# A two-layer decoder step: sampled tokens' queries spread by repeated copies and full transposes, not through DRAM

## The chip, the cores and the metric

The kernel runs on one core of one Trainium2 chip. The metric is the device time of one execution in microseconds; the kernel before took 1097.1 us, the median of three runs from 1093.85 to 1100.27.

## What is computed

The reference is one inference step of two decoder layers over 256 prompt tokens and 32 sampled tokens (8 sequences of 4). Each layer has one input projection, dilated window attention in three groups of four heads beside a spatial gate, an output projection, cross-attention to 256 memory tokens, and an MLP. The sampled tokens attend to cached keys and values:

```python
def decoder_layer(x, pos, past_kv, mem_k, mem_v, p):
    proj = x @ p['w_in']
    q = rope_partial(proj[..., :a].reshape(B, T, N_ATT_HEADS, HEAD_DIM), pos)
    k = rope_partial(proj[..., a:2 * a].reshape(...), pos)
    ...
    for gi, (win, dil) in enumerate(DIL_PATTERNS):      # (128, 1), (512, 4), (2048, 16)
        past = past_kv[gi]
        kv_all = jnp.concatenate([past, new_kv], axis=1)
        o, lse = dilated_window_attention(q[:, :, hs], kv_all[:, :, 0], kv_all[:, :, 1], n_prefix, win, dil)
    ...
    mixed = jnp.concatenate([att, sgu], -1) @ p['w_mix_out']
    x = layer_norm(DEEPNORM_ALPHA * x + mixed, p['ln1_g'], p['ln1_b'])
```

## The kernel before

All activations are held transposed: features on partitions, 288 tokens (256 prompt, 32 sampled) along a row. TensorE multiplies each 128x128 block of a weight three times, since float32 is put together from high and low halves: `linear` issues L336, L337 and L338 for each of eight blocks, 24 matmuls for a part of 128 columns. The halves of the weights are made two parts ahead, `wh` on ScalarE (L318) and `wl` on VectorE (L319), from `wraw`, which SP's queue loads.

The first phase of a layer is the input projection: 22 parts, first the queries q0 to q5 and keys k0 to k5 (two parts to a group of four heads), then values and gate. The rotation of q and k goes over two engines: VectorE shuffles and multiplies (L671, L672), GpSimd multiplies and adds (L673, then L674, here its two halves). Beside `linear` run the attention's generators, which the class `Tasks` interleaves on TensorE by costs and latencies that each step yields. The program order so made, and the tile framework's own estimate of when operands are ready, set the order of each engine's queue; at run time every engine takes its queue strictly in order.

The change lies in `decode_scores`, the attention of sampled tokens to cached keys. For the dilated groups 1 and 2, `query(g)` lays the queries out so that partition (b, c) holds the four queries of sequence b: two narrow transposes (L989) into PSUM, a copy `qn` to SBUF (L991), a store to the DRAM tile `qd` from ScalarE's queue (L993), and a load from it into `qb` on SP's queue (L996), which repeats each sequence's 4 KB over 16 partitions. A cache tile `cu` is then multiplied by `qb`, on GpSimd (L1007) or VectorE (L1009), and VectorE sums over each head's 64 elements (L1010); `zs` (L1016) and 16 or 8 small matmuls (L1022) bring the scores into the softmax. `query(2)` is called after tile 4 of group 1. Cache tiles come through a stream of five buffers on SP's queue, keys first; a buffer is free when its sum is done. After the softmax, L1043 to L1051 transpose the probabilities and `decode_pv` multiplies them by the cached values (L1075), 13 of whose loads can only be issued as buffers come free there. The keys of a group are also transposed for the outputs (L752, L768) and used for prompt scores (L850, L854) and scores of new tokens (L949); these need the second half of the keys' rotation. The first input of the output projection that needs the decode attention is `attH` (L1111).

Of the kernel before, what the change touches and what calls it, by code (L numbers as in the profile page):

```python
# [9 lines left out]
F32 = mybir.dt.float32  # L10
# [60 lines left out]
def constants():  # L71
    """Tables that depend on the shapes alone."""
# [10 lines left out]
    n = np.arange(32)  # L83
# [22 lines left out]
class Null:  # L106
    """Stands in for the context while the order of the loads is recorded."""
# [17 lines left out]
class Stream:  # L125
    """Loads in the order in which they are asked for, issued ahead of their use."""
# [6 lines left out]
    def issue(self, n=1):  # L133
        """Up to n more loads, as far as there are free buffers."""
        if self.recording:
            return
        while n and self.issued < min(len(self.order), max(self.pos - 1, 0) + self.bufs):
            t = self.pool.tile(self.shape, F32, name=self.tag, tag=self.tag, bufs=self.bufs)
            for dst, src in self.source(t, self.order[self.issued]):
                self.nc.sync.dma_start(out=dst, in_=src)  # L140
            self.tiles[self.issued] = t
            self.issued += 1
            n -= 1
# [12 lines left out]
class Tasks:  # L156
    """Interleaves generators on the tensor engine's queue.

    A task yields (cost, latency): the tensor-engine time that it has just issued, and how long its next step
    has to wait for the results; or the name of a flag to wait for.  `now` is the time issued so far."""  # L160
# [54 lines left out]
def build(ctx, tc, I, O, worder, corder, recording):  # L215
# [4 lines left out]
    dp = ctx.enter_context(tc.tile_pool(name="dp", bufs=1, space=bass.MemoryType.DRAM))  # L220

    # ---- tiles
# [27 lines left out]
    # ---- loads  # L250
# [36 lines left out]
    def behind(ins, name):  # L287
        """Queues an instruction behind the latest urgent one of that engine."""
# [34 lines left out]
    def weights(key):  # L323
        """The next 128 columns, with the splits running two such parts ahead."""
# [16 lines left out]
    def linear(name, l, k0, tiles, H, L, N, evac, norm=None, folded=0, apply_at=1, ks=range(KT)):  # L341
        """tiles: column tiles of 256; evac(n, ps, bias) with n the index of the 128-column half.

        The first `folded` tiles run on the input that `norm` has not normalised yet."""
# [24 lines left out]
    # ---- constants  # L369
# [41 lines left out]
    def diag(z, base, outer, n_outer, inner, n_inner, last=1):  # L411
        """z flat: elements base + outer*i + inner*j + (0..last-1), as [p, i, j, last]."""
# [5 lines left out]
    if recording:  # L418
        diag = lambda *a: nc  # noqa: E731
# [3 lines left out]
    # ---- input  # L423
# [13 lines left out]
    # ---- layer norm parameters, one column per (norm, g or b, layer, tile)  # L437
# [30 lines left out]
    class LN:  # L468
        """z = xres + partial results, then the norm over all features of each token.

        The first two tiles give a first estimate c of the mean; sums run over z - c."""
# [9 lines left out]
        def fold_input(self, n):  # L481
            """(z - c) * g, and g and b as two more columns."""
# [14 lines left out]
        def fold(self, ps):  # L497
            """What the normalised input gives, without its constant, and the constant."""
# [73 lines left out]
        def apply(self, H, L=None):  # L572
            """x into xres and, if given, split into H and L."""
# [20 lines left out]
    class LastNorm:  # L594
        """z = xres + partial results, then the norm with tokens on partitions, into the outputs.

        The three token tiles start at 0, 128 and 160; of the last one only the sampled tokens count."""
# [58 lines left out]
    def gelu(dst, ps):  # L656
        """gelu(ps), tanh form: x * (1 + tanh u) / 2 = x / (1 + exp(-2 u))."""
# [21 lines left out]
    def layer(l, xH, xL, norm):  # L679
# [10 lines left out]
        # small per-layer parameters  # L690
# [55 lines left out]
        def natural(g, kv):  # L746
            """Keys or values of one head group, tokens on partitions, for the outputs (and P V)."""
# [33 lines left out]
        # ---- spatial gate  # L781
# [56 lines left out]
        # ---- prompt self-attention, two head slots at a time  # L838
# [70 lines left out]
        # ---- decode self-attention; score rows are 16 b + 4 t + h  # L909
# [14 lines left out]
        def decode_scores():  # L924
# [58 lines left out]
            def query(g):  # L983
                """The queries of one group on the partitions that hold keys of their sequence."""
                for pr in range(2):
                    yield f"q{2 * g + pr}"
                ps = tr()
                for pr in range(2):
                    T.transpose(ps[0:32, 128 * pr:128 * pr + 128], qT[:, 2 * g + pr, 256:288], ident)  # L989
                qn = sb.tile([32, 256], F32, name="qn", tag="qn", bufs=2)  # L990
                S.copy(qn, ps[0:32, 0:256])  # L991
                qd = dp.tile([32, 256], F32, name=f"qd{g}", tag=f"qd{g}", bufs=1)
                nc.scalar.dma_start(out=qd, in_=qn)  # L993
                qb[g] = sb.tile([128, 1024], F32, name="qb", tag="kt", bufs=2)
                src = qd.rearrange("(b t) c -> b (t c)", t=4)[:, None, :].to_broadcast([8, 16, 1024])
                nc.sync.dma_start(out=qb[g], in_=src)  # L996

            yield from query(1)
            yield 200, 4000
# [114 lines left out]
        # ---- phase 1: input projection  # L1114
# [25 lines left out]
        # ---- phase 2: output projection of the mixers  # L1140
# [21 lines left out]
        # ---- phase 3: keys and values of the memory, cross-attention  # L1162
# [46 lines left out]
        def values(h):  # L1209
            """Values of the memory for one head, memory tokens on partitions."""  # L1210
# [156 lines left out]
        # ---- phase 4: squared-ReLU MLP in four slices of the hidden width  # L1367
# [84 lines left out]
```

## Time and profile before

| | |
|---|---|
| median of three runs | 1097.1 us |
| runs | 1093.85 to 1100.27 us |
| span of the profiled execution | 1090.5 us (its own time is not given) |
| TensorE busy | 1045.1 us |
| VectorE, ScalarE, GpSimd busy | 767.2, 534.1, 191.2 us |

The span runs from the first to the last instruction that the profiler saw. An engine's row in a timeline gives the start, the duration, the operation with its tiles, and in brackets how long the engine had been idle before it and what ended that idle time. Matmuls overlap, so their starts, not their durations, tell their pace. Layer 0's input projection and decode attention lie at 20 to 145 us, layer 1's at 565 to 685 us.

### The profile page before, as it was taken

The page shows a single profiled execution, that of the slowest core. Times are in us where ns is not written, and L with a number is a line of the kernel's source. Part 1 is how long each engine was busy: PE and PEld are TensorE (multiplying, and loading weights), DVE is VectorE, ACT ScalarE, POOL GpSimd, SP SyncE. Part 2 cuts the span into 40 slices and gives each one's busy share as a digit, 9 for nine tenths or more (in the row PEclk, how much of TensorE's full clock was granted, in tenths as well). Part 3 has the DMA queues.
Part 4 walks back from the last instruction along what each step waited for, and adds up shares of the span by engine and source line. Part 5 has one row for each costly group of instructions (what it writes and reads, how often), then busy time and mean ns, then how long its engine had stood idle before and what let it go on. Part 6 is the DMA issues. An engine that isn't in the chain of part 4 may idle for free. (4 is left out here: it accounts for less than half of the span.)

```text
span 1090.5 us, 20141 instructions
## 1 busy us (share of the span) xinstructions
PE 1045.1 (96%) x8038; PEld 957.0 (88%) x8038; DVE 767.2 (70%) x1406; ACT 534.1 (49%) x1000; POOL 191.2 (18%) x151
## 2 busy tenths in 40 slices
PE   8989999999999999999978998999999999999995
PEld 7979599878898999999968885997788999999995
DVE  6688689755479756565998876895554997565656
ACT  4437456544457535353553373674343585354432
POOL 5592022000023000000469300220000320000000
PEclk9999999999999999999989999999999999999998
DMA  9988955687854655545446869456865555555531
GB/s 291 303 249 280 244 185 189 205 256 236 299 160 136 194 161 186 156 157 172 136 128 214 250 209 265 155 192 201 276 209 206 155 146 184 160 171 183 182 117 43
DMA packets 185533, 213.68 MB, mean 196 GB/s; under 512 B 5760, under 2 KB 175136, under 8 KB 185440
## 3 DMA queue, kind: packets, MB, share of 16 engines
q1 hardware_dynamic: 177216, 205.00, 59.9%
q10 hardware_dynamic: 8224, 7.41, 2.1%
q8 instruction: 63, 1.03, 0.4%
q14 instruction: 30, 0.25, 0.1%
HBM read 203.80 MB, written 8.59 MB: 195 GB/s over the span
## 5 line engine op out<-in xcount | busy, mean ns | idle before, releaser
L318 ACT ACTIVATE wh<-wraw 128x1024 fp32r<-128x1024 f32 (+1 forms) x237 | 249.4, 1054 | 294.9 <-PE acc L337 218.8
L319 DVE TENSOR_TENSOR wl<-wraw,wh 128x1024 fp32r<-128x1024 f32 (+1 forms) x237 | 309.1, 1306 | 113.2 <-ACT wh L318 112.1
L336 PE MATMUL acc<-xH,wh 128*128 128x288 f32 x728 | 218.5, 301 | 6.8 <-DVE fy L502 6.8
L338 PE MATMUL acc<-xH,wl 128*128 128x288 f32 x728 | 217.5, 299 | 3.3 <-DVE wl L319 3.3
L337 PE MATMUL acc<-xL,wh 128*128 128x288 f32 x728 | 217.5, 299 | 0.0
L336 PE MATMUL acc<-hH,wh 128*128 128x288 f32 x512 | 151.3, 296 | 0.0
L337 PE MATMUL acc<-hL,wh 128*128 128x288 f32 x512 | 151.2, 295 | 0.0
L338 PE MATMUL acc<-hH,wl 128*128 128x288 f32 x512 | 150.9, 295 | 0.0
L336 PEld LDWEIGHTS acc<-xH,wh 128*128 128x128 f32 x728 | 138.6, 191 | 8.2 <-issue 5.2
L338 PEld LDWEIGHTS acc<-xH,wl 128*128 128x128 f32 x728 | 138.5, 191 | 4.8 <-DVE wl L319 4.2
L337 PEld LDWEIGHTS acc<-xL,wh 128*128 128x128 f32 x728 | 138.6, 190 | 1.0 <-DVE fy L726 0.4
L520 POOL TENSOR_TENSOR s<-s,xres 128x288 f32<-128x288 f32 x15 | 20.3, 1353 | 464.4 <-DVE s L516 463.9
L336 PEld LDWEIGHTS acc<-hH,wh 128*128 128x128 f32 x512 | 96.3, 188 | 0.0
L337 PEld LDWEIGHTS acc<-hL,wh 128*128 128x128 f32 x512 | 96.3, 188 | 0.0
L338 PEld LDWEIGHTS acc<-hH,wl 128*128 128x128 f32 x512 | 96.2, 188 | 0.0
L336 PE MATMUL acc<-fH,wh 128*128 128x290 f32 x256 | 78.1, 305 | 1.8 <-DVE fy L502 1.8
L337 PE MATMUL acc<-fL,wh 128*128 128x290 f32 x256 | 77.0, 301 | 0.0
L338 PE MATMUL acc<-fH,wl 128*128 128x290 f32 x256 | 75.7, 299 | 0.5 <-DVE wl L319 0.5
L336 PEld LDWEIGHTS acc<-fH,wh 128*128 128x128 f32 x256 | 48.3, 189 | 2.6 <-PE acc L338 2.2
L337 PEld LDWEIGHTS acc<-fL,wh 128*128 128x128 f32 x256 | 48.5, 190 | 0.9 <-DVE fL L494 0.2
L338 PEld LDWEIGHTS acc<-fH,wl 128*128 128x128 f32 x256 | 48.1, 189 | 1.2 <-DVE wl L319 1.0
L1007 POOL TENSOR_TENSOR cu<-cu,qb 128x1024 f32<-128x1024 f32 x15 | 44.1, 2956 | 11.1 <-DMA qb<-qd 10.7
(318 smaller groups left out, 2199.4 us busy)
## 6 DMA issues: line engine op xcount, KB each, us to landing
cu<-cache_mem_kv SPq DMA_DIRECT2D x64, 512.0 KB, 6.2
wraw<-w_up SPq DMA_DIRECT2D x32, 1024.0 KB, 5.5
wraw<-w_down SPq DMA_DIRECT2D x32, 1024.0 KB, 4.9
cu<-cache_kv_w SPq DMA_DIRECT2D x48, 512.0 KB, 6.4
wraw<-w_in SPq DMA_DIRECT2D x21, 1024.0 KB, 6.7
wraw<-w_xkv SPq DMA_DIRECT2D x16, 1024.0 KB, 5.6
wraw<-w_mix_out SPq DMA_DIRECT2D x8, 1024.0 KB, 6.0
wraw<-w_xq SPq DMA_DIRECT2D x8, 1024.0 KB, 5.0
```

The costliest lines, as they stand in the source:

```text
L318: S.activation(h[:, r], raw[:, r], AF.Copy)
L319: gates[f"split{k}"] = behind(V.tensor_sub(lo[:, r], raw[:, r], h[:, r].bitcast(F32)), "dve")
L336: m = T.matmul(ps, wh[:, k], H[:, k], start=first, stop=False)
L337: T.matmul(ps, wh[:, k], L[:, k], start=False, stop=False)
L338: T.matmul(ps, wl[:, k], H[:, k], start=False, stop=last)
L520: eng.tensor_add(self.s, self.s, xres[:, n])
L1007: G.tensor_mul(cu, cu, qb[g])
```

## The change

`query(g)` no longer goes through DRAM. ScalarE writes each of the two query tiles of a group (128 features x 32 tokens) into a tile `qx` in which every column is repeated 16 times, ordered by token, sequence and copy (two copies of 128x512, in the shared staging buffers `stg`). Eight full 128x128 transposes of these into two PSUM tiles then give rows that are already repeated over the partitions, and two 128x512 copies on ScalarE put them into `qb`. The costs that are yielded to the interleaving change, and the DRAM pool `dp` is gone. Elsewhere in the file only comments and docstrings differ.

```diff
-    dp = ctx.enter_context(tc.tile_pool(name="dp", bufs=1, space=bass.MemoryType.DRAM))
...
             def query(g):
...
                 for pr in range(2):
                     yield f"q{2 * g + pr}"
-                ps = tr()
+                qb[g] = sb.tile([128, 1024], F32, name="qb", tag="kt", bufs=2)
+                qx = []
                 for pr in range(2):
-                    T.transpose(ps[0:32, 128 * pr:128 * pr + 128], qT[:, 2 * g + pr, 256:288], ident)
-                qn = sb.tile([32, 256], F32, name="qn", tag="qn", bufs=2)
-                S.copy(qn, ps[0:32, 0:256])
-                qd = dp.tile([32, 256], F32, name=f"qd{g}", tag=f"qd{g}", bufs=1)
-                nc.scalar.dma_start(out=qd, in_=qn)
-                qb[g] = sb.tile([128, 1024], F32, name="qb", tag="kt", bufs=2)
-                src = qd.rearrange("(b t) c -> b (t c)", t=4)[:, None, :].to_broadcast([8, 16, 1024])
-                nc.sync.dma_start(out=qb[g], in_=src)
+                    qx.append(stg("qx"))
+                    src = qT[:, 2 * g + pr, 256:288].rearrange("p (b t) -> p t b", t=4)
+                    S.copy(qx[pr].rearrange("p (t b c) -> p t b c", t=4, b=8),
+                           src[:, :, :, None].to_broadcast([128, 4, 8, 16]))
+                yield 0, 1200
+                for i in range(2):
+                    ps = tr()
+                    for j in range(4):
+                        t, pr = 2 * i + j // 2, j % 2
+                        T.transpose(ps[:, 128 * j:128 * j + 128], qx[pr][:, 128 * t:128 * t + 128], ident)
+                    S.copy(qb[g][:, 512 * i:512 * i + 512], ps)
+                yield 900, 0

             yield from query(1)
-            yield 200, 4000
+            yield 0, 1500
```

The engines' queues come out in another order at three places that matter below. In the changed file the lines up to the query stand one line higher (L672 and L673 are the two halves of the rotation on GpSimd there, L318 the split of weights on VectorE) and those after it four lower (L1011 and L1013 are the multiplications, L1014 the sum, L1020 `zs`).

On GpSimd in layer 0, around the first multiplications by the query tile. Before (qT from 509 and 510 is q4, from 571 and 572 q5; kT from 615 and 616 is k2, from 655 and 656 k3):

```order
L674 TENSOR_TENSOR qT_156<-ro_509,ro_510 128x288
L673 TENSOR_TENSOR ro_572<-ro_572,const_63 128x288
L674 TENSOR_TENSOR qT_156<-ro_571,ro_572 128x288
L673 TENSOR_TENSOR ro_616<-ro_616,const_63 128x288
L674 TENSOR_TENSOR kT_157<-ro_615,ro_616 128x288
L673 TENSOR_TENSOR ro_656<-ro_656,const_63 128x288
L674 TENSOR_TENSOR kT_157<-ro_655,ro_656 128x288
L1007 TENSOR_TENSOR cu_253<-cu_253,qb_432 128x1024
L1007 TENSOR_TENSOR cu_340<-cu_340,qb_432 128x1024
L1007 TENSOR_TENSOR cu_377<-cu_377,qb_432 128x1024
L1007 TENSOR_TENSOR cu_516<-cu_516,qb_432 128x1024
```

All rotations up to k3 stand ahead of the multiplications here. On GpSimd in layer 0, the same place now (q4 is 515 and 516, q5 577 and 578, k2 621 and 622, k3 661 and 662):

```order
L673 TENSOR_TENSOR qT_154<-ro_515,ro_516 128x288
L1011 TENSOR_TENSOR cu_251<-cu_251,qb_423 128x1024
L1011 TENSOR_TENSOR cu_338<-cu_338,qb_423 128x1024
L1011 TENSOR_TENSOR cu_375<-cu_375,qb_423 128x1024
L1011 TENSOR_TENSOR cu_522<-cu_522,qb_423 128x1024
L672 TENSOR_TENSOR ro_578<-ro_578,const_61 128x288
L672 TENSOR_TENSOR ro_622<-ro_622,const_61 128x288
L1011 TENSOR_TENSOR cu_583<-cu_583,qb_423 128x1024
L672 TENSOR_TENSOR ro_662<-ro_662,const_61 128x288
L673 TENSOR_TENSOR qT_154<-ro_577,ro_578 128x288
L673 TENSOR_TENSOR kT_155<-ro_621,ro_622 128x288
L1011 TENSOR_TENSOR cu_627<-cu_627,qb_423 128x1024
```

Four multiplications have moved ahead of the rotations of q5, k2 and k3, and a fifth ahead of the second halves of q5 and k2.

On VectorE in layer 1, around the first product and sums of group 2 (st_6909 before, st_6984 now). Before:

```order
L1009 TENSOR_TENSOR cu_6759<-cu_6759,qb_6757 128x1024
L1029 ISA dp_6437,dm_7108<-sc_6176,const_63 128x224
L1029 ISA dm_7108 128x1
L1010 TENSOR_REDUCE st_6909<-cu_6711 128x16
L319 TENSOR_TENSOR wl_6945<-wraw_6674,wh_6944 128x1024
L1016 TENSOR_TENSOR zs_6861<-st_6527,const_63 128x1024
```

The split `wl` stands behind group 2's product and its first sum. On VectorE in layer 1 now:

```order
L1014 TENSOR_REDUCE st_6549<-cu_6692 128x16
L1033 ISA dp_6451,dm_7195<-sc_6190,const_61 128x224
L1033 ISA dm_7195 128x1
L318 TENSOR_TENSOR wl_6945<-wraw_6696,wh_6944 128x1024
L1020 TENSOR_TENSOR zs_6928<-st_6549,const_61 128x1024
L318 TENSOR_TENSOR wl_7010<-wraw_6696,wh_7009 128x1024
```

Two splits and `zs` of group 1 have moved ahead of them.

On SP's queue in layer 1, around the last loads of cached values (w2048) and the memory's rows `mem_nat`. Before:

```order
L140 DMA cu_7512<-cache_kv_w2048 64x4x256 x2
L140 DMA cu_7554<-cache_kv_w2048 64x4x256 x2
L140 DMA cu_7575<-cache_kv_w2048 64x4x256 x2
L140 DMA cu_7582<-cache_kv_w2048 64x4x256 x2
L1142 DMA mem_nat_7643<-mem_prompt 128x2x1024
```

The memory's rows come last. On SP's queue in layer 1 now:

```order
L140 DMA cu_7591<-cache_kv_w2048 64x4x256 x2
L140 DMA cu_7598<-cache_kv_w2048 64x4x256 x2
L140 DMA cu_7605<-cache_kv_w2048 64x4x256 x2
L1146 DMA mem_nat_7673<-mem_prompt 128x2x1024
L140 DMA cu_7612<-cache_kv_w2048 64x4x256 x2
```

The load of the memory's rows has moved ahead of the last tile's two halves.

## Rows read from the trace of the kernel before

**Rows 1.** Page: span, then busy time, share and instructions of TensorE

```profile
span 1090.5 us, 20141 instructions
...
PE 1045.1 (96%) x8038; PEld 957.0 (88%) x8038; DVE 767.2 (70%) x1406; ACT 534.1 (49%) x1000; POOL 191.2 (18%) x151
```

**Rows 2.** Timeline of ScalarE, layer 0: start, us, engine, line, operation, out<-in [idle before]

```profile
34.53 0.36 ACT L991 COPY qn<-tr 32x256 f32<-32x256 f32 x1 [0.28 <-PE tr L989]
...
38.23 0.35 ACTq L993 DMA_DIRECT2D qd<-qn  x1
...
38.62 0.59 ACT L712 COPY wst<-tr 128x512 f32<-128x512 f32 x1 [3.73 <-PE sc L932]
```

**Rows 3.** Timeline of the SP queue, layer 0

```profile
44.30 0.71 SPq L996 DMA_DIRECT2D qb<-qd  x1
```

**Rows 4.** Timeline of GpSimd (POOL), layer 0

```profile
42.79 1.67 POOL L674 TENSOR_TENSOR qT<-ro 128x288 f32<-128x288 f32 x1
...
49.13 1.66 POOL L674 TENSOR_TENSOR kT<-ro 128x288 f32<-128x288 f32 x1
...
55.93 12.38 POOL L1007 TENSOR_TENSOR cu<-cu,qb 128x1024 f32<-128x1024 f32 x4 [1.93 <-DMA qb<-qd]
```

**Rows 5.** View of the tile qb: duration ns min/median/max; idle us before it, times

```profile
L1007 POOL TENSOR_TENSOR cu<-cu,qb x15: 2347/3362/3457, 55.9 to 615.6; 128x1024 f32<-128x1024 f32 x15
...
  DMA qb<-qd: 13.9, 5
```

**Rows 6.** Waits of TensorE, 20 to 145 us: us in total, times, longest

```profile
PE tr L752 <- POOL kT L674: 2.9, 2, 1.8
...
PE tr L850 <- DVE m L858: 0.7, 1, 0.7
```

**Rows 7.** Timeline of TensorE, layer 1

```profile
595.72 0.40 PE L989 MATMUL tr<-const,qT 128*32 128x128 f32 x1 [3.06 <-POOL qT L674]
...
596.15 0.44 PE L338 MATMUL acc<-xH,wl 128*128 128x288 f32 x1
...
596.39 0.44 PE L336 MATMUL acc<-xH,wh 128*128 128x288 f32 x1
...
619.12 0.61 PE L338 MATMUL acc<-xH,wl 128*128 128x288 f32 x1 [2.64 <-DVE wl L319]
...
676.38 0.64 PE L1075 MATMUL o<-cu,z 128*32 128x256 f32 x8 [1.64 <-DMA cu<-cache_kv_w]
```

**Rows 8.** Timeline of GpSimd, layer 1

```profile
575.67 1.67 POOL L674 TENSOR_TENSOR qT<-ro 128x288 f32<-128x288 f32 x1
...
578.93 9.17 POOL L1007 TENSOR_TENSOR cu<-cu,qb 128x1024 f32<-128x1024 f32 x3 [1.60 <-DMA qb<-qd]
...
595.63 0.80 POOL L674 TENSOR_TENSOR kT<-ro 128x288 f32<-128x288 f32 x1
```

**Rows 9.** Timeline of VectorE, layer 1

```profile
615.70 1.22 DVE L1010 TENSOR_REDUCE st<-cu 128x16 f32<-128x1024 f32 x1 [1.97 <-POOL cu L1007]
```

**Rows 10.** Timeline of TensorE, layer 0

```profile
44.18 0.38 PE L336 MATMUL acc<-xH,wh 128*128 128x288 f32 x1
...
57.07 0.38 PE L989 MATMUL tr<-const,qT 128*32 128x128 f32 x2
...
57.29 0.60 PE L752 MATMUL tr<-const,kT 128*128 128x128 f32 x4
...
57.72 0.38 PE L768 MATMUL tr<-const,kT 128*32 128x128 f32 x2
```

**Rows 11.** Busy times of a stretch, granted clock (PEclk), DMA share, GB/s

```profile
595.80:597.80 2.00, 2.00 (x10) 1.92 (x11) 2.00 (x5) 0.36 (x1) 1.92 (x3) 0.50 0.21 35
```

**Rows 12.** Timeline of the SP queue, layer 1

```profile
652.01 14.69 SPq L140 DMA_DIRECT2D cu<-cache_kv_w  x13
...
667.19 0.37 SPq L1142 DMA_DIRECT2D mem_nat<-mem_prompt  x1
```

**Rows 13.** Busy times in layer 1, DMA share and GB/s last

```profile
664.00:668.00 4.00, 4.00 (x26) 2.07 (x26) 3.04 (x13) 2.08 (x9) 0.00 (x0) 1.00 1.14 200
```

## The prediction

> **What bounds the kernel now.** I read the page first: TensorE is busy for 1045.1 of 1090.5 us [rows 1], so its queue is the length of the kernel, and only what lengthens that queue or leaves it idle counts. The profiled span lies 6.6 us under the median of 1097.1 us; the time of that execution itself is not given, so I add my sum, made against the span, to the median. Then I read TensorE's timeline over the two stretches in which the queries are spread (20 to 145 us in layer 0, 565 to 685 us in layer 1), for every idle time above 0.2 us and its releaser, then each releaser's own engine. The reader is to see three things.
>
> First, the removed chain is long. In layer 0 the copy of the queries stands at 34.53, its store is issued at 38.23 [rows 2], the load at 44.30 [rows 3], and GpSimd's first multiplication with it begins at 55.93 [rows 4]. Engines wait 13.9 us for these loads, in 5 places [rows 5].
>
> Second, hardly any of that is TensorE's. Its waits in layer 0 are 2.9 us for rotated keys and 0.7 us for VectorE [rows 6]. The rotated keys come from GpSimd, whose queue also holds the multiplications.
>
> Third, in layer 1 two waits do hang on the chain. TensorE waits 3.06 us for q5's rotation [rows 7], which stands on GpSimd behind multiplications that waited for the load until 578.93 [rows 8]. It waits 2.64 us for a weight split [rows 7], which stands on VectorE behind a sum that waited for GpSimd's product, 1.97 us, that had waited for group 2's load [rows 9]. Behind either wait the matmuls start 0.24 us apart [rows 7]; before, 96 of them took 44.18 to 57.07, 0.134 us each [rows 10]. The granted clock of that slow stretch is 0.50 [rows 11], so it is the lower of the two levels (1.2 for 2.4 GHz). By the spacing it lasts 10 to 12 matmuls, which at 0.106 us more each is 1.1 us behind the first wait and 1.25 behind the second.
>
> **The work added to TensorE.** Per layer 16 full transposes come and 4 narrow ones go. Four full ones start at 57.29 and the next instruction at 57.72 [rows 10], 0.11 each, so 16 cost 1.75. Two narrow ones take 0.22 (57.07 to 57.29 [rows 10]), so 4 give back 0.44. Three more breaks in the rows of matmuls at about 0.09 each add 0.27. Sum +1.6 us per layer, 3.2 in all, all on the path. A transpose here is dearer by the Trainium skill, TensorE: Matmul & The Clock Gate, Part 4: PE-mode transpose, which gives about 275 ns for one in a kernel (for bf16). By that figure 32 of them would cost 8.8 us and the forecast below would be 5.3 us longer; the rows above, at 0.11 in a row, speak against it, and I use them.
>
> The ScalarE copies (4 per group, 0.59 us for 128x512 [rows 2]) cost TensorE nothing: ScalarE is a part ahead with its splits. If that cover were gone, 16 copies would be 9.4 us. The copy of q5's queries waits on ScalarE for GpSimd's q5, with a split queued behind it; that split is wanted two parts, 6.4 us, later, so I take nothing. The stores and loads themselves (2 each per layer, 512 KB for each load) free SP's and ScalarE's queues; TensorE waited for neither, so nothing.
>
> **Layer 0: the order on GpSimd.** The scheduler, which now thinks that the query tile is ready early, moves four multiplications ahead of the rotations of q5, k2 and k3. Before, k2 is done at 50.8 [rows 4], long before TensorE wants it. Now it comes behind this row:
> - TensorE reaches the six transposes of group 1 at about 44.4 [rows 10] and needs 0.7; two copies follow on ScalarE between its other work: the query tile is ready at 46.2 (45.4 to 47.5), after q4's rotation has ended at 44.46 [rows 4].
> - Four multiplications: 12.4 us as before [rows 4], so to 58.6. Bounds: 4 x 2.35 = 9.4 and 4 x 3.46 = 13.8 [rows 5].
> - The first halves of q5 and k2, a fifth multiplication (2.35 to 3.46), k3's first half, then the second halves of q5 and k2. A half takes 0.81 to 1.67 us (1.66 and 1.67 in [rows 4], 0.80 in [rows 8]). Middle 8.4, ends 6.4 and 10.5. So k2 is there at 67.0 (61 to 71).
>
> TensorE gets to the group that needs k2 one part after 57.07 [rows 10]: 57.07 + 3.2 + 1.0 for eight transposes and two breaks = 61.3. It waits 5.7 us, and 1.2 for the clock behind it. k3 follows on GpSimd a sixth multiplication and two halves later, 4.9 us, while TensorE has 3.7 us of work: another 1.2. Sum 8.1, in place of the 3.6 of [rows 6] (k4 and k5, which now come before they are wanted): +4.5.
>
> Behind this, VectorE's sums wait for GpSimd's products with splits queued behind them. I walked that queue: the split that is wanted first comes 0.4 to 2 us before TensorE needs it, so +0.4, ends 0 and +2. With 1.6 of work layer 0 is at **+6.5** (-1.5 to +10) when the values of the caches begin; two pairs of prompt scores that move ahead of that point (0.42 each) leave the stretch behind it, so they cancel.
>
> The spread of 2.35 to 3.46 us for one multiplication [rows 5] has a rule beside it: the Trainium skill, SBUF — State Buffer, Who interferes with whom, says that GpSimd and a VectorE instruction with two SBUF inputs exclude each other for a whole instruction. By it the four would take 9.4 us if VectorE did only sums and waits in that time, and 13.8 if it split weights all along. The trace agrees with both ends, and VectorE has three splits in those 12 us as before, so the middle stays.
>
> **Layer 1.** GpSimd's order does not change, and q4's second half runs from 575.67 to 577.34 whatever the query does [rows 8]; the tile, ready at about 574, lets the multiplications start at 577.4 instead of 578.93. So all behind moves up 1.5 us, and no more: k2 (which ends at 596.43 [rows 8]) is there at 594.9, and TensorE, 0.8 later by added transposes, comes at about 593.4. It waits 1.5 instead of 3.06 and stays under the length at which the clock fell: -2.7. The second wait (2.64 and 1.25 for the clock behind it) goes, since VectorE now has the split ahead of group 2's products: -3.9. Work +1.6. Sum -5.0.
>
> What is late next: the values of the caches. TensorE ends that stretch with a wait of 1.64 us for the last of them [rows 7]. Thirteen loads are issued from 652.01 on, the memory's rows (1 MB) behind them at 667.19 [rows 12]. Now the memory's rows are issued ahead of the last tile. 1 MB at the 200 GB/s of that time [rows 13] would be 5.2 us; if the two share the engines, little. I take 2.5 (0 to 5). And three pairs of prompt scores (0.42 each) move ahead of the stretch, which loads bound, so 1.3 is not given back. Layer 1: -5.0 + 1.3 + 2.5 = **-1.2** (-5 to +2).
>
> **Sum.** +6.5 - 1.2 = +5.3; I take 5 us, so 1102 us.
>
> **Rivals.**
> - *Rotations not late, faster.* If the four multiplications take 9.4 and each half 0.8, k2 comes at 46.2 + 9.4 + 6.4 = 62.0: a wait of 0.7, none for k3. Layer 0 is then 0.7 + 1.6 - 3.6 = -1.3, layer 1, with the memory's rows hidden and the moved scores given back, -5.0: 1097.1 - 6.3 = 1091. For it: 2.35 us is on record [rows 5]. Against: three splits of VectorE fall in that time.
> - *Slower.* VectorE becomes the bound in layer 0: its sum of the first product waits for GpSimd, and k2's rotation on VectorE, two splits and the second sum stand behind it. It decides once the query tile comes later than about 48, when the split for the part at 58 is late: then 2 us more on TensorE, k2 later by the same 2, and with the memory's rows fully ahead (5 instead of 2.5) the sum is 5.3 + 2 + 2 + 2.5 = 11.8, so 1109; with one of these 1105 to 1107. For it: margins of 0.4 us in my walk. Against: the copies on ScalarE are short.
> - *It does not do what it says.* The products start no earlier, because the fifth cache tile or q4 holds GpSimd in both layers (as q4 does in layer 1). Then the order on GpSimd gives back about what layer 1 wins, and 3.2 us of work less 3 to 4 of the two old waits is left: 1096 to 1098.
>
> **How the numbers follow.** The forecast, 1102, has 0.43 with a range of its own of 1098 to 1106; the limit of +0.5% (about what a measurement here can tell from no change, 5.5 us) is 1102.6, so I put 0.30 of it within and 0.13 above. Faster rival 0.17. Slower rival 0.26, the dearer transposes 0.02. No effect 0.12. So faster 0.17, same 0.30 + 0.12 = 0.42, slower 0.13 + 0.26 + 0.02 = 0.41. For 8 in 10 the range leaves out the outer half of the faster rival and the outer third of the slower: 1090.5 to 1108.5.
>
> **What would show it.** In the changed kernel's timeline: GpSimd's four multiplications from about 46 to 59; k2's second half at 65 to 69; TensorE idle 4 to 7 us for GpSimd's keys near 61 to 67, with 0.24 us between the matmuls behind it; in layer 1 one wait of 1 to 2 us for k2 near 594, no wait for a split near 619, and a wait of 2 to 6 us for the last cache values near 674. A query tile later than 50, no wait near 61, or a wait for the split in layer 1 would make me wrong.

## The result, and the profile after

The changed kernel took 1116.51 us (median; 1114.37 to 1118.29), the kernel before beside it 1098.68 us (1093.85 to 1100.67): a ratio of 1.0158, 95% interval 1.0123 to 1.0193. It is slower by 1.6%, where 1102 us and at most 1108.5 were forecast. The profiled execution took 1115.4 us. Its page, against [rows 1]:

```profile
span 1113.7 us, 20180 instructions
...
PE 1063.1 (95%) x8062; PEld 972.0 (87%) x8062; DVE 770.3 (69%) x1406; ACT 541.2 (49%) x1012; POOL 187.5 (17%) x151
```

The span grew by 23.2 us, TensorE's busy time by 18.0: most of the loss is not idle time. Four stretches hold nearly all of it. They are cut at the same places of TensorE's queue in every kernel: in layer 0 from the 51st group of three matmuls of `linear` to the first multiplication with cached values, and from there to the 201st group; in layer 1 from the 977th group, and to the 1153rd. The view gives the busy time of each engine by stretch; the columns are the stretch, its length, the busy times, the granted clock (PEclk), DMA share and GB/s. The kernel before:

```profile
41.00:111.75 70.75, 67.08 (x497) 63.38 (x496) 60.13 (x114) 36.64 (x79) 41.62 (x21) 1.00 0.89 272
111.75:153.68 41.93, 39.35 (x331) 27.40 (x330) 26.80 (x93) 17.14 (x43) 0.00 (x0) 0.96 0.83 239
564.87:651.31 86.44, 80.12 (x595) 74.65 (x593) 72.50 (x132) 40.35 (x82) 41.30 (x26) 0.96 0.69 213
651.31:696.48 45.17, 42.33 (x351) 30.47 (x350) 30.10 (x97) 21.13 (x51) 1.86 (x2) 1.00 0.82 234
```

The changed kernel:

```profile
41.83:122.61 80.78, 76.38 (x521) 70.89 (x520) 61.91 (x120) 39.75 (x83) 38.21 (x21) 0.92 0.69 223
122.61:172.45 49.84, 42.57 (x322) 28.29 (x322) 25.74 (x85) 17.54 (x46) 0.00 (x0) 0.83 0.75 202
584.16:671.68 87.52, 85.22 (x618) 79.64 (x616) 75.59 (x140) 44.45 (x89) 40.92 (x26) 0.94 0.61 198
671.68:719.85 48.17, 41.34 (x338) 30.84 (x338) 27.99 (x88) 20.39 (x50) 1.87 (x2) 0.93 0.78 219
```

The length less TensorE's busy time is its idle time. The four stretches grew by 10.0, 7.9, 1.1 and 3.0 us, 22.0 in all; idle time accounts for +0.7, +4.7, -4.0 and +4.0, together 5.4, and busy time for the other 16.6. The added work was put at 3.2 us. The third column from the end tells where most of the rest is: the granted clock fell from 1.00, 0.96, 0.96 and 1.00 to 0.92, 0.83, 0.94 and 0.93. The levels are 1.00 and 0.50 (2.4 and 1.2 GHz), so twice what is missing from 1.00 is the share of a stretch at the lower one: by that 47 us of the four stretches, against 10 before.

TensorE's timeline in layer 0, where it waits for k2 (columns as in [rows 7]):

```profile
62.81 0.29 PE L336 MATMUL acc<-xL,wh 128*128 128x288 f32 x1
67.51 0.48 PE L751 MATMUL tr<-const,kT 128*128 128x128 f32 x1 [4.41 <-POOL kT L673]
...
70.54 0.44 PE L335 MATMUL acc<-xH,wh 128*128 128x288 f32 x1
70.78 0.44 PE L336 MATMUL acc<-xL,wh 128*128 128x288 f32 x1
...
76.05 0.38 PE L335 MATMUL acc<-xH,wh 128*128 128x288 f32 x1
```

and GpSimd's timeline ahead of it, which answers to [rows 4]:

```profile
46.92 11.46 POOL L1011 TENSOR_TENSOR cu<-cu,qb 128x1024 f32<-128x1024 f32 x4 [2.20 <-ACT qb L999]
58.33 2.55 POOL L672 TENSOR_TENSOR ro<-ro,const 128x288 f32<-128x288 f32 x2
60.84 2.40 POOL L1011 TENSOR_TENSOR cu<-cu,qb 128x1024 f32<-128x1024 f32 x1
...
65.69 1.77 POOL L673 TENSOR_TENSOR kT<-ro 128x288 f32<-128x288 f32 x1
```

So the mechanism stands as it was drawn: four multiplications from 46.92 to 58.38, k2's second half ending at 67.46, one wait of 4.41 us. Behind it the matmuls start 0.24 us apart (70.54, 70.78), not for ten of them but up to 75.3. The clock of that stretch and of one in the next, in the same columns as above:

```profile
65.10:75.30 10.20, 7.79 (x29) 6.97 (x30) 10.20 (x13) 1.11 (x3) 10.12 (x8) 0.50 0.74 240
133.40:147.00 13.60, 12.02 (x56) 5.11 (x55) 2.65 (x11) 4.08 (x12) 0.00 (x0) 0.50 1.13 203
```

The second of these follows three waits for cached values in a row, and one for `od`, the output of the decode attention on its way to `attH`, comes after it:

```profile
129.79 0.64 PE L1079 MATMUL o<-cu,zp 128*32 128x256 f32 x8 [0.89 <-DMA cu<-cache_kv_w]
132.42 0.64 PE L1079 MATMUL o<-cu,zp 128*32 128x256 f32 x8 [1.99 <-DMA cu<-cache_kv_w]
...
135.07 1.08 PE L1079 MATMUL o<-cu,zp 128*32 128x256 f32 x8 [1.47 <-DMA cu<-cache_kv_w]
...
156.05 0.41 PE L1100 MATMUL tr<-const,od 128*128 128x128 f32 x2 [2.12 <-DVE od L1093]
```

In layer 1 there is one wait for k2, none for a split, and a late last tile of cached values, with a wait for `attH` behind it; at 0.50 lie 614.62 to 621.45 and 699.96 to 706.78:

```profile
613.75 0.33 PE L751 MATMUL tr<-const,kT 128*128 128x128 f32 x1 [2.30 <-POOL kT L673]
...
698.60 0.64 PE L1079 MATMUL o<-cu,z 128*32 128x256 f32 x8 [2.69 <-DMA cu<-cache_kv_w]
...
703.18 1.09 PE L335 MATMUL acc<-attH,wh 128*128 128x288 f32 x3 [1.28 <-ACT attH L1115]
```

### The profile page after: what moved, and what is told of

It reads as the page before. It is cut to its first block, busy times and chain, and to the rows that moved or that the text cites. A ratio compares the mean times of both kernels' runs of the same rounds, so it can differ in the third digit from the quotient of the medians.

```text
span 1113.7 us, 20180 instructions
## 1 busy us (share of the span) xinstructions
PE 1063.1 (95%) x8062; PEld 972.0 (87%) x8062; DVE 770.3 (69%) x1406; ACT 541.2 (49%) x1012; POOL 187.5 (17%) x151
## 5 line engine op out<-in xcount | busy, mean ns | idle before, releaser
L318 DVE TENSOR_TENSOR wl<-wraw,wh 128x1024 fp32r<-128x1024 f32 (+1 forms) x237 | 307.4, 1300 | 121.7 <-ACT wh L317 121.1
L1011 POOL TENSOR_TENSOR cu<-cu,qb 128x1024 f32<-128x1024 f32 x15 | 40.5, 2723 | 24.2 <-ACT qb L999 24.2
```

What stands on the lines that cost most here:

```text
L318: gates[f"split{k}"] = behind(V.tensor_sub(lo[:, r], raw[:, r], h[:, r].bitcast(F32)), "dve")
L1011: G.tensor_mul(cu, cu, qb[g])
```

## The experiments

Two questions lead through them: what the waits and the clock behind them cost, and which of the change's two parts, the new way of the data or the new yields, brings them.

**GpSimd's rotations first.** The multiplications are held behind the rotations that the program asks for before them:

```diff
-        (G if ROPE[1] else V).tensor_add(dst, e, f)
+        gates["rope"] = (G if ROPE[1] else V).tensor_add(dst, e, f)
...
-                        G.tensor_mul(cu, cu, qb[g])
+                        behind(G.tensor_mul(cu, cu, qb[g]), "rope")
```

> The changed kernel, with one thing put back: a multiplication by the query tile on GpSimd is queued behind the rotations issued so far, so q5, k2, k3 and k4 stand between the first four multiplications. Theory (the late rotation of k2 is what costs layer 0): no wait of TensorE near 61 to 67, no slow clock there, layer 0's projection 7 to 9 us shorter than in the changed kernel, which took 1116.5; time 1106 to 1110. Rival (the transposes and copies themselves cost it, whatever GpSimd's order): the stretch stays within 2 us and the time at 1114 to 1118.

Measured: 1108.49 us, 1.0107 times before (1.0042 to 1.0172). The time lies where the theory had it, but the stretch does not. The wait of 4.41 us is gone, and others have come. The waits of TensorE in layer 0 (line, releaser: us in all, times, longest):

```profile
PE s L1026 <- DVE zs L1020: 2.9, 1, 2.9
PE tr L767 <- DVE m L857: 2.4, 1, 2.4
PE sc L948 <- POOL kT L673: 1.7, 1, 1.7
```

The stretch up to the cached values took 83.47 us, more than the 80.78 of the changed kernel. What this kernel gains lies behind it: 44.92 and 45.24 us in the second and fourth stretches, against 49.84 and 48.17. The edit moved more than GpSimd's queue there: the four prompt scores that the changed kernel leaves for layer 0's second stretch now stand ahead of it, and in layer 1 the memory's rows are loaded behind all loads of cached values again. So without the late rotation of k2 the first stretch is as long as with it; that GpSimd's order by itself is not the loss is shown further down, with the old yields.

**TensorE kept busy in the wait.** 46 matmuls whose result is overwritten stand ahead of k2's transposes in layer 0:

```diff
-            ps = tr()
+            ps = tr(); [T.matmul(ps[:, 0:288], xH[:, 0, 0:128], xH[:, 0], start=True, stop=True) for _ in range(46 if (g, kv, l) == (1, 0, 0) else 0)]
```

> The changed kernel with 46 useless matmuls of 128x288 (6.1 us at full clock) put on TensorE in layer 0 ahead of the transposes that need k2, to fill the wait of 4.4 us. Theory (most of that wait's price is the lower clock behind it, 10.2 us at half pace): the clock stays at its upper level from 61 to 75, and the projection of layer 0 gets 1 to 3 us shorter although 6.1 us of work are added. Rival (the clock would have fallen anyway, because of the row of short matmuls): the added work costs 1.7 us or more and a stretch at the lower level stays near 65 to 75.

Measured: 1113.43 us, 1.015 times before (1.0066 to 1.0234). TensorE's timeline at the wait, and the clock of the whole stretch:

```profile
57.81 6.23 PE L748 MATMUL tr<-xH 128*128 128x288 f32 x46
...
66.12 0.33 PE L751 MATMUL tr<-const,kT 128*128 128x128 f32 x1 [1.43 <-POOL kT L673]
...
67.80 0.29 PE L335 MATMUL acc<-xH,wh 128*128 128x288 f32 x1
67.93 0.29 PE L336 MATMUL acc<-xL,wh 128*128 128x288 f32 x1
...
71.59 0.38 PE L335 MATMUL acc<-xH,wh 128*128 128x288 f32 x1
```

```profile
42.00:119.60 77.60, 75.97 (x563) 71.11 (x563) 61.75 (x118) 39.88 (x83) 37.07 (x20) 1.00 0.70 223
```

The same instructions, from k2's first transpose to the part behind k3's, take 71.59 - 66.12 = 5.5 us at the full clock (0.2 of it a wait for k3) and 76.05 - 67.51 = 8.5 us in the changed kernel: the clock behind that wait cost 3.1 us, not 1.2. The stretch up to the cached values fell from 80.78 to 78.84 us although 6.1 us of work (57.81 to 63.87) was put in and its idle time shrank by no more than 2.8 (4.4 to 1.6). So the clock, at 1.00 in all of it and without the 13.6 us at 0.50 of the changed kernel, gave back some 5 us: 0.3 to 0.4 us for each us at the lower level. The Trainium skill, TensorE: Matmul & The Clock Gate, HAM oscillation — how this bites in real kernels, counts half of the time at the lower clock as lost. Behind this wait it was 3.1 of 10.2 us, so the measurement decides for less: 2.4 us of these had passed in the wait itself (65.1 to 67.5).

**The memory's rows last.** In layer 1 `mem_nat` had been issued between the loads of cached values:

```profile
672.38 9.83 SPq L140 DMA_DIRECT2D cu<-cache_kv_w  x11
682.27 0.60 SPq L1146 DMA_DIRECT2D mem_nat<-mem_prompt  x1
684.76 1.68 SPq L140 DMA_DIRECT2D cu<-cache_kv_w  x2
```

The load is put behind the last of them (the lines that keep hold of that load are left out):

```diff
...
-        nc.sync.dma_start(out=mem_nat, in_=I["mem_prompt"][0].rearrange("(a p) d -> p a d", p=128))
+        behind(nc.sync.dma_start(out=mem_nat, in_=I["mem_prompt"][0].rearrange("(a p) d -> p a d", p=128)), "g2.1")
```

> The changed kernel with the load of the memory's rows held behind the last load of cached values, as it stood before. Theory (the 1 MB ahead of the last tile costs layer 1's end): the wait of 2.69 us for the last values falls to about 1, the lower clock behind it goes, layer 1's end is 3 to 5 us shorter, time 1112 to 1114. Rival (those loads share the engines, so the order does not matter): layer 1's end stays within 1 us and the time at 1116.

Measured: 1106.58 us, 1.0092 times before (1.0057 to 1.0126). The SP queue:

```profile
668.49 14.09 SPq L140 DMA_DIRECT2D cu<-cache_kv_w  x13
683.13 0.37 SPq L1146 DMA_DIRECT2D mem_nat<-mem_prompt  x1
```

The fourth stretch fell from 48.17 to 44.92 us, below the 45.17 of before; the last wait for cached values is 1.73 instead of 2.69 us, and the one for `attH` is gone. So of the loss some 3 us by the trace hang on this one load. The median moved by 10 us, below what either theory had said; the traced execution took 1109.98, 3.4 more than the median, and its stretches of layer 0 are unchanged (80.36 and 49.60), so I don't put the rest of that down to the load.

**The yields of before.** The data path is the new one, the three yields are the old:

```diff
-                yield 0, 1200
...
-                yield 900, 0
...
             yield from query(1)
-            yield 0, 1500
+            yield 200, 4000
```

> The changed kernel with the costs and latencies that the query steps yielded before (one latency of 4000 behind the first query, none between copies and transposes). Theory (the order on GpSimd comes from the estimate of when the query tile is ready, not from these costs): the four multiplications still stand ahead of q5, k2 and k3, the wait near 61 to 67 stays 4 to 6 us, time 1112 to 1120. Rival (the smaller latency made the order): the wait goes and the time falls to 1106 to 1110.

Measured: 1091.95 us, 0.9952 times before (0.9922 to 0.9983): faster than the kernel before, by half a per cent. I had expected 1112 to 1120. The four stretches, from the fastest of its ten executions:

```profile
40.62:114.67 74.05, 69.28 (x514) 65.59 (x512) 63.47 (x112) 39.10 (x83) 39.21 (x21) 0.98 0.77 245
114.67:155.68 41.01, 38.92 (x331) 27.59 (x330) 27.15 (x93) 17.50 (x45) 0.00 (x0) 1.00 0.83 245
566.42:647.70 81.28, 78.58 (x598) 74.35 (x596) 72.97 (x130) 43.62 (x88) 41.71 (x26) 0.98 0.68 213
647.70:691.94 44.24, 41.38 (x359) 30.62 (x358) 30.55 (x100) 20.62 (x51) 1.86 (x2) 1.00 0.79 239
```

GpSimd still has the four multiplications ahead of k2's rotation, and nearly at the same times:

```profile
45.71 10.46 POOL L1009 TENSOR_TENSOR cu<-cu,qb 128x1024 f32<-128x1024 f32 x4 [2.20 <-ACT qb L998]
...
63.47 0.80 POOL L673 TENSOR_TENSOR kT<-ro 128x288 f32<-128x288 f32 x1
```

The first stretch has as much idle time as in the changed kernel (4.8 against 4.4 us), but in pieces of 2.35 us and less, and its clock is 0.98 against 0.92. On SP's queue the memory's rows come behind the cached values again, so that move came from the yields and not from the query's way. On TensorE 36 prompt-score matmuls stand ahead of the cached values in either layer, as before the change; the changed kernel has 44 in layer 0 and 48 in layer 1, and its transposes for group 2 in layer 0 stand 9 to 41 groups of three matmuls later.

**The old way of the data with the new yields.** The other corner of the square: the kernel before, with the three new yields at the same places.

```diff
+                yield 0, 1200
                 ps = tr()
...
                 nc.sync.dma_start(out=qb[g], in_=src)
+                yield 900, 0
...
             yield from query(1)
-            yield 200, 4000
+            yield 0, 1500
```

> The kernel before, store and load through DRAM kept, with the three yields of the change put at the same places of its generator (0, 1200 ahead of the transposes of the queries, 900, 0 behind the load, 0, 1500 in place of 200, 4000 after group 1). Theory (the yields, not the data path, make the time: they move pairs of prompt scores and the group's transposes to other places of TensorE's queue, which leaves less work between the cached values and more and longer stretches at the lower clock): slower than before by 0.8 to 2%, 1106 to 1120 us, with waits of over 4 us in all for the cached values and lower-clock stretches of over 25 us in the four stretches that the queries touch. Rival (the transposes and GpSimd's early multiplications make the time): within 0.5% of before, 1091 to 1103 us.

Measured: 1114.77 us, 1.0156 times before (1.0109 to 1.0204), just what the whole change costs, and within the theory's range. Its four stretches:

```profile
42.89:113.42 70.53, 69.27 (x518) 64.67 (x516) 62.61 (x121) 36.91 (x79) 40.84 (x21) 1.00 0.83 259
113.42:162.82 49.40, 39.23 (x312) 27.01 (x310) 24.63 (x82) 16.85 (x42) 0.00 (x0) 0.86 0.82 202
574.31:670.74 96.43, 84.04 (x611) 77.73 (x609) 74.96 (x142) 41.58 (x85) 39.95 (x26) 0.93 0.66 191
670.74:719.74 49.00, 40.81 (x336) 29.07 (x334) 27.90 (x87) 19.90 (x48) 1.86 (x2) 0.93 0.78 216
```

The loss looks different here: idle time is 1.3, 10.2, 12.4 and 8.2 us, 32.0 in all against 15.4 before, with the longest wait 5.22 us for cached values in layer 0, and the first stretch loses nothing. What the two kernels share are the second and fourth stretches (49.4 and 49.0 here, 49.8 and 48.2 in the changed kernel) and their lower clock.

**Each inner yield alone.** The changed kernel without the `yield 900, 0`, and without the `yield 0, 1200`. The third yield decides nothing: with 200, 4000 in its place beside the two inner ones, the queues of all engines are built the same.

> The changed kernel without its second yield (900, 0, behind the eight transposes of a group); 0, 1200 stays. The order on TensorE in layer 0 keeps the late place of group 2's transposes and the four more prompt-score matmuls ahead of the cached values; layer 1 has two of six back. Theory (the latency of 0, 1200 does most of it): 1108 to 1116 us. Rival (the cost of 900, which the planner takes for work that is not there, does it): 1090 to 1100 us.

> The changed kernel without its first yield (0, 1200, between the copies and the transposes of a group); 900, 0 stays. Group 2's transposes move forward and prompt scores stand as before the change. Theory (the latency does most of it): 1090 to 1100 us. Rival (the cost of 900 does it): 1108 to 1117 us.

Measured: 1104.95 us without the cost (ratio 1.0084, 1.0054 to 1.0115), 1110.08 without the latency (1.0134, 1.0086 to 1.0181). The first lies between the two theories' times, the second in the rival's: neither yield does it alone, and each of them alone leaves the kernel slower than before. Without the latency the prompt scores stand as before the change, and still the first stretch takes 81.2 us, with waits of 3.31 us for k2 and 2.85 for `zs`. So the moved scores are not the one cause either. The four stretches took 80.36, 50.38, 84.00 and 43.62 us without the cost, and 81.22, 44.92, 81.52 and 49.05 without the latency: in these traces taking the cost away shortens layer 1 alone, and taking the latency away the second and third stretches. Only with both do the memory's rows stand among the loads of cached values; without either one of them they come last.

**Both good edits together.** The yields of before and the memory's rows last.

> The changed kernel with the yields of before (none within the query, 200, 4000 after group 1) and with the memory's rows loaded behind the last tile of cached values. With the order by the old yields the kernel took 1091.95 us; the late load took 3 us off the wait at the end of layer 1 where the yields were the new ones. Theory (the two add): 1087 to 1091 us. Rival (with the old yields the memory's rows stand behind the last tile anyway or hide): 1090.5 to 1093.5 us, no difference.

Measured: 1089.64 us, 0.9957 times before (0.9932 to 0.9981). The median lies in the theory's range, but the ratio is that of the old yields alone, so nothing was added. With the old yields the memory's rows already stand behind the thirteen loads: there was nothing left to gain.

**The new yields in one layer.** `if l == 1:` (or `l == 0`) ahead of the new yields, the old ones in the other layer.

> The changed kernel with the yields of before in layer 0 and the new ones in layer 1 alone. With the old yields in both layers it took 1091.95 us, with the new in both 1116.51. Theory (each layer pays for its own order; by the two traces 15.5 us of the difference lie in layer 0 and 10.1 in layer 1): 1100 to 1104 us, with layer 0 as with the old yields (cached values from about 115 us on, first parts of the next stretch at 156) and layer 1 as in the changed kernel. Rival (the loss is one thing that starts in layer 0 and drags on): 1090 to 1094 us.

> The changed kernel with the new yields in layer 0 alone, those of before in layer 1. Theory (each layer pays for its own order): 1105 to 1109 us, the sum of its gain and that of the kernel with new yields in layer 1 alone is the whole difference of 24.6 us. Rival (loss starts in layer 0 and drags on): 1113 to 1118 us.

Measured: 1099.81 us with the new yields in layer 1 (ratio 1.0042, 1.0009 to 1.0074), just under the theory's range, and 1106.88 in layer 0 (1.0111, 1.0078 to 1.0145). Above the 1091.95 with none that is 7.9 and 14.9 us, 22.8 together, of the 24.6 with both (by the ratios 0.9 and 1.6%, 2.5 together, of 2.1). Each layer pays for its own order. The traces say it by stretch: with the new yields layer 0 took 80.38 and 48.64 us (80.78 and 49.84 in the changed kernel), with the old ones 74.05 and 42.48; layer 1 took 85.97 and 49.68 with the new (87.52 and 48.17), 82.53 and 47.68 with the old.

**Rotations first, with the old yields.** The edit of the first experiment on the kernel with the old yields.

> The changed kernel with the yields of before, and GpSimd's multiplications put behind the rotations of q and k that stand before them in the program, as in the kernel before. Theory (with the yields of before, GpSimd's order is not what costs; the wait that it takes away, 2.4 to 4.8 us in layer 0, is replaced by one for products or splits): 1089 to 1096 us. Rival (the multiplications ahead of the rotations still cost the waits and the clock behind them): 1083 to 1088 us.

Measured: 1091.81 us, 0.9967 times before (0.9945 to 0.999), against 1091.95 without the edit. So with the old yields GpSimd's order costs nothing. Once more one wait took the place of another: the longest of layer 0, 2.35 us for a weight split, is gone, and TensorE now waits 2.7 us for keys at another line.

```profile
PE sc L948 <- POOL kT L673: 2.7, 1, 2.7
```

**More work among the cached values.** By now I held that the stretch from the first to the last multiplication with cached values is as long as its loads take, so that work in it is free. Fifteen matmuls were added there, to the kernel with the old yields:

```diff
+                    if (l, g) == (0, 1) and i in (1, 2, 3):
+                        fill = tr()
+                        for _ in range(5):
+                            behind(T.matmul(fill[:, 0:256], zn[:, 0], zn.rearrange("p a n -> p (a n)"),
+                                            start=True, stop=True), "o3")
                     yield 520, 1500
```

> The changed kernel with the yields of before, and in layer 0 fifteen added matmuls (zeros of 128x128 by 128x256, into a tile nobody reads) between the multiplications with the cached values: about 3 us of TensorE work (15 by about 0.2). The stretch from the first to the last of these multiplications was 25.4 us with the old yields, 26.2 before the change, with twelve halves of prompt scores in it, and 28.5 in the changed kernel with four. Theory (the stretch is as long as its 13 loads take, so what stands in it is hidden, and what an order moves ahead of it or behind it is paid in full): the stretch stays at 24.5 to 26.5 us and the kernel at 1090 to 1094. Rival (TensorE's own work sets the stretch): 28 to 29 us and 1094 to 1097.

Measured: 1101.29 us, 1.0051 times before (1.0024 to 1.0077). The trace has two records for each of these matmuls, so five took 2.43 us and not 1; the three lots are 7.3 us:

```profile
126.03 2.43 PE L1086 MATMUL tr<-zn 128*128 128x256 f32 x10
```

The stretch without them, and with them:

```profile
114.67:140.09 25.42, 23.72 (x218) 12.96 (x217) 16.57 (x65) 12.28 (x37) 0.00 (x0) 1.00 0.83 219
```

```profile
115.79:151.38 35.59, 33.90 (x248) 20.33 (x247) 15.89 (x62) 12.52 (x36) 0.00 (x0) 0.95 0.79 231
```

It grew by 10.2 us, more than the work added and more than even the rival had said (28 to 29 us for the stretch). My theory falls: with 23.72 of 25.42 us busy, TensorE sets this stretch nearly as much as the loads do. What is put in lengthens it; why by 2.9 us more than its own length is not shown.

## Why the prediction was wrong

**What the runs settle.** Two ways of the data and two sets of yields make a square, each as a ratio to the kernel before: old way and old yields 1, new way and old yields 0.9952, old way and new yields 1.0156, new way and new yields 1.0158. The intervals of the last two, 1.0109 to 1.0204 and 1.0123 to 1.0193, lie far from the first two. The new way gains half a per cent; the yields, which the section on the change names in one sentence, lose 1.6% on the old way of the data and 2.1% on the new (0.9952 to 1.0158). Whether still other numbers would do better than the old ones was not tried. The prediction never asked what the yields do by themselves. It took the new order of the queues, priced the pieces that it saw move, and charged them to the query's earlier arrival. Two steps of its sum failed: the price of the lower clock behind a wait, and layer 0's stretch of cached values, which was left out of the sum.

**Right.** The four multiplications (46 to 59 said, 46.92 to 58.38), k2's second half (67.0 said, 67.46) and one wait for it (5.7 said, 4.41, since TensorE came at 63.1 and not at 61.3; the second one, for k3, did not come). The upper end of the sum up to k2 was made too low: five halves and a multiplication of the rows named give 11.8 us and not 10.5; measured were 9.1. The added transposes start 0.11 to 0.13 us apart, as priced. In layer 1 the wait for a split is gone and k2's wait is 2.30 us (1.5 said). The memory's rows ahead of the last tile made a wait there (2.5 us of loss taken, 3.25 given back by moving the load). The first stretch of layer 1 was put at -5.0 without the moved scores, and with the old yields it went from 86.44 to 81.28, -5.2; part of that is luck, since eight matmuls of the prompt's attention with its values, which the sum did not count, had moved behind it. The "slower" rival reached 1109 by way of VectorE; TensorE waits for no split in layer 0, so its mechanism did not come.

**Wrong: the term for the clock.** "1.2 for the clock behind it" was sized on the two stretches of the trace of before. Behind k2's wait it was 3.1 us, and the lower clock lasted 10.2 us, not the 2.6 or so that the pace of ten to twelve matmuls had given. In layer 1 the wait for k2, put at 1.5 us and so at nothing for the clock, was 2.30 us and was followed by 6.8 us at 0.50. There the first stretch was to become 3.7 us shorter, with the moved scores, and became 1.1 longer: its idle time fell by 4.0, as the terms for the two waits have it (4.2), but its busy time grew by 5.1 instead of some 0.5, with 10.2 us at the lower clock where none was forecast. By the rate of the second experiment, 0.3 to 0.4, the 37 us more at the lower clock in the four stretches are an estimated 11 to 15 us of the 16.6 that busy time grew by; the added work is a few us (in the first stretch of layer 0 TensorE is busy for 67.08 us before, and for 69.28 at a clock of 0.98 with the old yields). The kernel before says the same by itself: over its 78 executions beside the experiments the mean clock ranged from 0.972 to 0.987, and by a straight line through them the span grew by some 0.4 us for each us more at the lower level; the changed kernel stood at 0.965 to 0.966 in all four.

**Wrong: "they cancel".** Two pairs of scores moved ahead were to leave the stretch of the cached values, and their length with them; nothing else was charged to it. They left (12 score matmuls there before, 4 now), and the stretch behind them grew by 7.9 us all the same: three waits for loads, 4.35 us in all, in place of a single one of 2.35, the one for `od`, and 17 us at the lower clock (0.83 granted over 49.84). With less work between the loads TensorE runs into them; the same is seen with the old way of the data (8.9 us of waits for cached values in layer 0, in four pieces). By the last experiment work there isn't free either: the loads and TensorE's queue are balanced to within some 2 us, and to move work out turns it into waits. That this balance, and not another piece of the order, makes the 7.9 us is my reading and not shown. Without the latency, with all twelve scores there as before, the stretch is 44.92 us, 3.0 above before; with GpSimd's rotations first, and none of the twelve left there, it is 44.92 too. So the scores alone do not set it.

**By the sum.** Layer 0: forecast +7.3 before the cached values, with the moved scores, and -0.8 behind; measured +10.0 and +7.9. Layer 1: forecast -3.7 and +2.5; measured +1.1 and +3.0. So the stretch behind layer 0's first cached values is the largest miss, 8.7 us, and layer 1's first stretch the next, 4.8. What stays open is which of the pieces that the two inner yields move counts how much; taking away either leaves a loss (1.0084 and 1.0134), so they don't add up.

## What to carry to other kernels

When a change touches both an operation and the numbers that place it in a queue, price the numbers apart: put the new numbers on the old code and the old numbers on the new code before either is judged. In a kernel whose TensorE is busy 95% of the time price a wait with the lower clock behind it: each wait above 2 us in the four stretches of the changed kernel (4.41, 2.12, 2.30, 2.69) was followed by 3.4 to 10.2 us at 0.50. The same idle time in pieces was not reliably cheaper: in layer 0's first stretch with the old yields 4.8 us of it went with a clock of 0.98 in one trace and 3.7 us with 0.91 in another, and behind three pieces close together, 4.35 us in all, 13.6 us ran at 0.50. And a moved filler may cost more than its own length. A cost that is right for an instruction (900 for eight transposes that take about 0.9 us) can still make a worse order: without it the changed kernel's ratio fell from 1.0158 to 1.0084.

## What was not expected of the hardware

The clock fell without a wait, too. In the changed kernel TensorE had no idle time above 0.2 us from 70 to 122 us, and yet, behind a row of short matmuls from 84.4 on, mostly transposes, scores and products 16 columns wide, the granted clock went to 0.50 from 88.98 to 92.38:

```profile
84.40:88.90 4.50, 4.50 (x33) 3.95 (x32) 2.01 (x6) 2.42 (x5) 2.30 (x1) 1.00 0.84 291
88.98:92.38 3.40, 3.40 (x16) 2.67 (x15) 2.31 (x10) 1.88 (x6) 3.40 (x3) 0.50 0.36 97
```

With the old yields there is a shorter row of this kind, and the clock stayed full around it in one trace (81.7 to 87.2 us) and fell in another, of the kernel with the memory's rows last, though TensorE's queue is the same there:

```profile
85.54:92.37 6.83, 6.58 (x29) 5.81 (x29) 6.83 (x20) 2.11 (x6) 0.00 (x0) 0.50 0.92 280
```

And how long it stays low differs, even for one queue and one wait: behind the wait of 4.4 us 10.2 us in the changed kernel and 6.8 with the memory's rows last, behind that of 2.35 us with the old yields 3.4 and 6.8 us in these two traces. The first stretch took 74.05 us in the one and 76.64 in the other. So a single trace is good to some 3 us for a stretch, and a lone difference of that size in the sections above says little. What sets it for one and the same queue is not shown by these runs.
